# A scheduled one-core hybrid block: lag products with their sides exchanged, x's transposes issued ahead, powers on POOL

## The chip, the cores and the metric

The kernel runs on one core of a Trainium2 chip. The metric is the device time of one execution in microseconds. The engines are called as in the profile: PE (TensorE products), PEld (its weight loads), DVE (VectorE), ACT (ScalarE), POOL (GpSimd), SP (SyncE, which here only issues DMAs).

## The reference

One layer over 2048 tokens of 1024 channels, f32:

```python
hn = rmsnorm(h, mix_norm_g)
u, g_ssm, q, k, v, g_attn = split(hn @ w_in)          # 512 columns each
y_ssm = s5_branch(u, ...) * silu(g_ssm)               # 32 groups of 16 channels, 64 complex states
y_att = stick_breaking(q, k, v) * silu(g_attn)        # 8 heads of 64, strictly causal
h = h + concat(y_ssm, y_att) @ w_out
h = h + sigmoid(rmsnorm(h) @ w_ple_gate) * (p @ w_ple_proj)
```

`s5_branch` turns the complex poles `exp(a dt)`, the input matrix B and the output matrix C into a linear recurrence over time, then applies GELU and a gated linear unit. The change lies in u, in the gate product of `g_ssm` and in the preparation of the recurrence.

## The kernel before

**Products.** Large products are done in three f32r products of high and low halves (`split`, `mm3`): an operand's high part is written by ACT, the low part by DVE.

**u stage (`phase_u`).** T = 0 to 7 are blocks of 256 tokens. For T of 1 and more `load_x` fetches two halves of x, squares them on ACT (`jk`, sum into `ss`), makes the row factor `rs_x` (DVE L73, then a power on POOL, L501), scales x on ACT (L604), turns it by 64-row transposes on PE (`ps_x`, L520), splits the result into `xt` (ACT L507, DVE L66) and writes `xt` to memory as `hn`. T = 0 comes turned from the host. For T = 0 and 1 (`RAW = 2`) x is not scaled; `norms` computes the row factors (`ps_row`, `e.row`) and u is multiplied by them afterwards (L641, on POOL). The u product (`ps_u`) of a T has 96 PE products in four banks, which ACT copies to `uq` (L639).

**Preparation (`ssm_chain`, `ssm_pack`).** `ssm_chain` makes, on tiles with 32 columns, `dt`, `mag`, sine and cosine (`small_exp`, `small_sincos`), the powers of the pole (`pr`, `pi`, by `cmul` in doubling steps of 1, 2, 4, 8 times 32 columns), the scaled input matrices `bb` and `bbs` and the tables `tabs`. The tables' products run on POOL (`cmul` with `aside=True`), the rest on DVE. A pack (eight, four groups each) forms `bn` from the powers on DVE (128 x 1024), turns it on PE into `mb` (`stB`), and multiplies `bn` with C into `lags`, which goes to memory (`lag`) and comes back as a Toeplitz operand.

**Gate and state-space stage.** Packs, `ssm_batch` and `gate_unit` (product `ps_sg`, banks o and z0, evicted by ACT and DVE) run interleaved; the first attention projections run there too. Attention, gated linear unit and output follow.

**Order.** A planner in the file sets the order of every engine's instructions: `plan` collects operations and dependences, `duration` gives each a cost, `list_schedule` takes on each engine the ready operation of lowest rank, `best_order` repeats that with ranks from a backward pass and keeps the plan with the earliest end, `arrange` fixes it. Hints change it: `e.first` puts operations before all others, `e.later(T)` holds DMAs until the operation marked by `e.mark(T)` has begun, `e.abreast` keeps a group together. Engines run their queues strictly in that order on the chip, whatever is ready.

Of the kernel before, what the change touches and what calls it, by code (L numbers as in the profile page):

```python
# [8 lines left out]
F32 = mybir.dt.float32  # L9
# [4 lines left out]
ALU = mybir.AluOpType  # L14
# [4 lines left out]
P = 128  # L19
# [30 lines left out]
HOLD = 2  # L50
ACT0 = True
RAW = 2
MARK0, MARK1 = 7, 6
MATB = 1
GSB = 2
# [9 lines left out]
def vt(nc, out, a, b, op):  # L65
    nc.vector.tensor_tensor(out, a, b, op=op)  # L66
# [109 lines left out]
def ssm_chain(e, keep, sm):  # L176
# [35 lines left out]
    pr = R.pr = kt("pwr", [L + 1, G])  # L212
    pi = R.pi = kt("pwi", [L + 1, G])
# [4 lines left out]
    n = 1  # L218
    while n < L:
        bc = [a[:, n].unsqueeze(1).to_broadcast([P, n, G]) for a in (pr, pi)]  # L220
        cmul(e, sm, pr[:, n + 1:2 * n + 1], pi[:, n + 1:2 * n + 1], pr[:, 1:n + 1], pi[:, 1:n + 1], *bc, [n, G])
        n *= 2
    R.pis = kt("pwis", [L + 1, G])
    vs(nc, R.pis, pi, nsgn, ALU.mult)
# [79 lines left out]
def ssm_pack(e, sm, R, b):  # L304

    nc = e.nc
    gs = slice(b * GB, (b + 1) * GB)
    sh = [P, GB, L, GH]
    bn = sm.tile(sh, F32, tag="bn", name="bn")
    tm = sm.tile(sh, F32, tag="tm", name="tm")  # L310

    def pw(a, lo, rev):
        v = a[:, lo:lo + L, gs].rearrange("p t g -> p g t")
        if rev:
            v = v[:, :, ::-1]
# [12 lines left out]
    gp = nc.gpsimd.tensor_tensor  # L328
    gp(cview, pw(R.pr, 1, False), st(R.cts), op=ALU.mult)
    gp(tm2, pw(R.pi, 1, False), st(R.ct2), op=ALU.mult)  # L330
    gp(cview, cview, tm2, op=ALU.subtract)
    bnf = bn.rearrange("p g (s i) h -> p (g s) (i h)", s=HS)
    mbf = mb.rearrange("p g s m -> p (g s) m")
    for q in range(GB * HS // 4):
        ps = e.bank("ps_pack", "w0", "w1")
        for k in range(4):
            nc.tensor.transpose(ps[:, k * P:(k + 1) * P], bnf[:, 4 * q + k], e.ident)
        nc.scalar.activation(mbf[:, 4 * q:4 * q + 4].rearrange("p g m -> p (g m)"), ps, AF.Copy)
    ps = e.bank("ps_pack", "w0", "w1")
    for s in range(HS):  # L340
        for k in range(GB):
            o = (s * GB + k) * GH
            nc.tensor.matmul(ps[:, o:o + GH], bnf[:, HS * k + s], R.cts[:, b * GB + k, :], start=True, stop=True)
    lags = sm.tile([P, HS + 1, GB, GH], F32, tag="lags", name="lags", bufs=2)
    nc.vector.memset(lags[:, HS], 0.0)
    nc.scalar.activation(lags[:, :HS], ps[:, :HS * GB * GH].rearrange("p (s g h) -> p s g h", s=HS, h=GH), AF.Copy)
# [193 lines left out]
def phase_u(e, pool, xp, chain):  # L540
# [50 lines left out]
    def load_x(T):  # L591
        xt = xp.tile([P, 2, 2, NC8, P], F32R, tag="xg", name="xt", bufs=2)
        for hf in range(2):
            t0 = (2 * T + hf) * P
            x = pool.tile([P, DM], F32, tag="x", name="x", bufs=XB)
            nc.sync.dma_start(x, e.x[0, t0:t0 + P, :])
            jk = e.spare.tile([P, DM], BF16, tag="part", name="jk", bufs=1)
            ss = pool.tile([P, 1], F32, tag="ss", name="ss", bufs=2)
            nc.scalar.activation(jk, x, AF.Square, accum_out=ss)
            if T < RAW:  # L600
                sums.append(ss)
            else:
                rs = rms_rstd(e, pool, ss, 1, DM, "x")
                nc.scalar.activation(x, x, AF.Copy, scale=rs)  # L604
            for h, ps in enumerate(turned(e, "ps_x", ("tr", "ssm") if hf else ("z0", "z1"), [x[:, c * P:(c + 1) * P] for c in range(NC8)])):
                d = slice(64 * h, 64 * h + 64)
                split(e, xt[:, hf, 0, :, d], xt[:, hf, 1, :, d], ps)
            nc.sync.dma_start(e.hn_d[2 * T + hf], xt[:, hf].rearrange("p s c t -> p (s c t)").bitcast(F32))
        return xt

    xts = {}
    with e.first():
        xts[0], w = load_plain(0)
        with e.later(0):
            xts[1] = load_x(1)
        norms()
    prep = chain()
    for T in range(NT // 2):
        if 2 <= T + 1 < NT // 2:
            xts[T + 1] = load_x(T + 1)  # L620
        xt = xts.pop(T - 2, None)
        xt = xts[T]
        if T % 4 == 0:
            uq = [pool.tile([P, L, NCH // 2], F32, tag="uq", name="uq", bufs=5) for ct in range(4)]
        ps = [e.bank("ps_u", "w0", "w1", "o", "acc")[:, :256] for _ in range(4)]
        if T == 2:
            e.mark(T)
        if T == 1:
            e.mark(3)
        for ct, c in [(ct, c) for c in range(NC8) for ct in range(4)] if T == 0 else [(ct, c) for ct in range(4) for c in range(NC8)]:  # L630
            if T == 0 and ct == 0 and c == MARK1:
                e.mark(1)
            cs = slice(ct * P, (ct + 1) * P)
            mm3(e, ps[ct], (w[c][:, 0, cs], w[c][:, 1, cs]), (xt[:, :, 0, c], xt[:, :, 1, c]), c == 0, c == NC8 - 1)
        n = NCH // 8
        for ct in range(4):
            k0 = (T % 4) * n
            o, out = ps[ct].rearrange("p (c j) -> p j c", j=L), uq[ct][:, :, k0:k0 + n]
            nc.scalar.activation(out, o, AF.Copy)  # L639
            if T < RAW:  # L640
                nc.gpsimd.tensor_tensor(out, out, e.row[T].rearrange("p (c j) -> p j c", j=L), op=ALU.mult)  # L641
            if T % 4 == 3:
                c0 = (T // 4) * (NCH // 2)
                nc.gpsimd.dma_start(e.u_d[ct][:, :, c0:c0 + NCH // 2].rearrange("j p c -> p j c"), uq[ct])
# [3 lines left out]
def gate_unit(e, pool, w, T, xt):  # L648
# [390 lines left out]
def hybrid_block_kernel(ctx: ExitStack, tc: tile.TileContext, x, xt, small, p, w_in, ssm_w_glu, w_out, w_ple_gate,  # L1039
# [94 lines left out]
    def hint(kind):  # L1134
# [2 lines left out]
        yield  # L1137
        rows.append((n, len(nc.cur_bb.bb.instructions), kind))

    e.first, e.later, e.mark = (lambda: hint("first")), (lambda T=2: hint(T)), (lambda T: rows.append((len(nc.cur_bb.bb.instructions), T, "mark")))  # L1140
    e.rows, e.abreast = rows, abreast
    e.wpool = pool(ctx, "w", 16)
# [128 lines left out]
def duration(i, name, outs, ins, psum):  # L1271
# [232 lines left out]

def best_order(ops, pre, soft, length, mode, rows, turns=6):

    first, last, inner, soon = set(), set(), set(), set()
    hints = [r for r in rows if len(r) == 3]
    mark = {T: a for a, T, kind in hints if kind == "mark"}
    for a, b, kind in hints:  # L1510
        for k in range(a, b):
            if kind == "first":
                soon.add(k)
            elif kind in mark and type(ops[k]).__name__ == "InstDMACopy":
                soft[k].add(mark[kind])
    for a, b in [r for r in rows if len(r) == 2] + [(k, k + 2) for k, i in enumerate(ops) if type(i).__name__ == "InstRegisterMove"]:
# [10 lines left out]
        return [r - 1e6 if k in inner and k not in heads else r for k, r in enumerate(rank)]  # L1527

    for _ in range(turns):
        order, start, done = list_schedule(ops, pre, soft, length, mode, lead([k - 1e5 if k in soon else r for k, r in enumerate(rank)], first))  # L1530
# [67 lines left out]
```

## Time and profile before

| | |
|---|---|
| median of 3 runs | 1563.97 us (1562.64 to 1567.96) |
| profiled execution | 1565.11 us, span 1563.4 us |
| granted TensorE clock, mean | 0.984 |
| POOL, DVE, ACT busy | 844.9, 1057.6, 931.2 us |

A group row gives: line, engine, operation, output and inputs, shapes, count | busy us, mean ns of one | idle time of the engine before them and what ended it. A wait row gives: who waited for whom, us in total, times, longest. A timeline row gives: start, duration, engine, line, operation, count, and the idle time before it.

### The profile page before, as it was taken

To read this page: it belongs to the slowest core of one execution; us is meant where nothing else is said; L and a number is where in the kernel's file an instruction comes from. 1 tells how busy PE (TensorE), PEld (TensorE's weight loads), DVE (VectorE), ACT (ScalarE), POOL (GpSimd) and SP (SyncE) were. 2 spreads that over 40 slices of the span, in tenths; PEclk is the share of its full clock that TensorE was granted. 3 is DMA by queue.
4 is the path that set the end of the run, shared out by engine and by line. 5 is a ranking of instruction groups with operands and counts; after the bars stand their busy time and mean duration, and the time that the engine had idled before them with its cause. 6 is when DMAs were issued, how large, how long until landed. Compare 5 with 4: busy or idle time off the path is not lost.

```text
span 1563.4 us, 34915 instructions
## 1 busy us (share of the span) xinstructions
PE 1484.2 (95%) x13120; PEld 1261.9 (81%) x13120; DVE 1057.6 (68%) x1953; ACT 931.2 (60%) x2069; POOL 844.9 (54%) x1131
## 2 busy tenths in 40 slices
PE   8899999889999999998999988999999999999998
PEld 7899989878888888887888876777776888777776
DVE  7845868657677877678768785666869556754544
ACT  6553545456677877677867777666765435633432
POOL 3843433435556666565666598774565654433433
PEclk9999999999999999999999998999999999999999
DMA  8767636454332422334223365763347645622211
GB/s 334 273 248 216 205 109 208 147 182 157 139 110 95 134 94 95 108 116 136 91 89 116 127 222 167 234 181 95 104 147 252 200 162 182 196 68 93 89 61 61
DMA packets 168377, 236.22 MB, mean 151 GB/s; under 512 B 63504, under 2 KB 109712, under 8 KB 156816
## 3 DMA queue, kind: packets, MB, share of 16 engines
q1 hardware_dynamic: 166272, 226.50, 44.4%
q0 software_dynamic: 1936, 7.49, 1.7%
q8 instruction: 104, 1.70, 0.5%
q14 instruction: 65, 0.53, 0.1%
HBM read 169.05 MB, written 64.90 MB: 150 GB/s over the span
## 4 chain that ended last, share of the span: by engine, by line
PE 77%; DVE 8%; ACT 5%; issue 4%; POOL 3%; DMA 2%; POOLq 0%; SPq 0%; ACTq 0%; DVEq 0%
PE ps_q L744 20%; PE ps_o L848 6%; PE ps_z L809 6%; PE ps_wt L520 4%; PE ps_g L713 3%; PE ps_g L715 3%; PE ps_h L713 3%; PE ps_h L714 3%; PE ps_g L714 3%; PE ps_h L715 3%; DVE px L825 2%; DMA wst<-in_ssm_w_glu_dram 1%; PE ps_sg L535 1%; PE ps_u L535 1%; PE ps_u L536 1%
## 5 line engine op out<-in xcount | busy, mean ns | idle before, releaser
L827 POOL TENSOR_TENSOR be<-be,px 128x512 f32<-128x512 f32 (+3 forms) x320 | 317.3, 996 | 205.8 <-DVE px L825 157.2
L744 PE MATMUL ps_q<-w_w,xt 64*128 64x512 f32 x2880 | 406.1, 404 | 11.4 <-DVE v L66 9.7
L825 DVE TENSOR_TENSOR_SCAN px<-px,ps_z 128x512 f32<-128x512 f32 (+3 forms) x320 | 339.8, 1086 | 103.5 <-ACT be L819 73.8
L744 PEld LDWEIGHTS ps_q<-w_w,xt 64*128 64x128 f32 x2880 | 297.5, 187 | 52.8 <-issue 9.5
L814 ACT ACTIVATE px<-ps_z 128x512 f32<-128x512 f32 (+3 forms) x320 | 162.8, 540 | 76.9 <-PE ps_z L809 58.8
L840 ACT ACTIVATE ws<-ps_wt 128x512 f32<-128x512 f32 (+3 forms) x320 | 164.9, 550 | 62.7 <-PE ps_wt L520 62.4
L819 ACT ACTIVATE be<-ps_z 128x512 f32<-128x512 f32 (+3 forms) x320 | 167.8, 555 | 0.5 <-PE ps_wt L520 0.5
L809 PE MATMUL ps_z<-k,q 64*128 64x512 f32 (+3 forms) x960 | 148.9, 384 | 14.0 <-DVE px L825 11.1
L848 PE MATMUL ps_o<-ws,v 128*64 128x128 f32 x2176 | 140.1, 281 | 1.0 <-ACT ws L840 1.0
L848 PEld LDWEIGHTS ps_o<-ws,v 128*64 128x64 f32 x2176 | 120.3, 139 | 19.6 <-issue 15.6
L520 PEld LDWEIGHTS ps_wt<-ident,be 64*128 64x128 f32 x2176 | 104.5, 142 | 28.8 <-POOL be L827 8.9
L809 PEld LDWEIGHTS ps_z<-k,q 64*128 64x128 f32 x960 | 97.1, 189 | 33.3 <-DVE px L825 17.3
L520 PE MATMUL ps_wt<-ident,be 64*128 64x64 f32 x2176 | 111.5, 229 | 8.0 <-ACT ws L840 3.2
L1020 POOL TENSOR_TENSOR sg<-sg,h 128x512 f32<-128x512 f32 x32 | 44.8, 1411 | 114.3 <-DVE sg L66 114.3
L501 POOL TENSOR_TENSOR rs_qk<-rs_qk,mhalf 128x4 f32<-128x4 f32 x64 | 65.7, 1027 | 42.4 <-DVE rs_qk L73 41.6
L535 PE MATMUL ps_u<-xt,w_w 128*128 128x256 f32 x256 | 75.9, 297 | 6.6 <-ACT w_w L485 6.1
L536 PE MATMUL ps_u<-xt,w_w 128*128 128x256 f32 x256 | 75.4, 295 | 2.1 <-DVE xt L66 2.1
L66 DVE TENSOR_TENSOR yr<-sx,yr 128x512 fp32r<-128x512 f32 x64 | 53.4, 854 | 34.9 <-ACT yr L507 34.1
L823 POOL TENSOR_SCALAR_AFFINE_SELECT px<-px 128x128 f32<-128x128 f32 x128 | 39.4, 318 | 69.1 <-ACT px L814 67.5
L537 PE MATMUL ps_u<-xt,w_w 128*128 128x256 f32 x256 | 74.6, 294 | 0.0
L507 ACT ACTIVATE yr<-sx 128x512 fp32r<-128x512 f32 x64 | 39.3, 628 | 52.1 <-POOL sx L906 20.5
L1014 ACT ACTIVATE sg<-sg,rs 128x512 f32<-128x512 f32 x24 | 17.4, 725 | 74.0 <-DVE sg L66 74.0
(421 smaller groups left out, 3694.9 us busy)
## 6 DMA issues: line engine op xcount, KB each, us to landing
xt<-hn SPq DMA_DIRECT2D x60, 1024.0 KB, 4.9
hn<-xt SPq DMA_DIRECT2D x16, 1024.0 KB, 8.5
h<-h SPq DMA_DIRECT2D x64, 256.0 KB, 3.5
wst<-in_w_in_dram SPq DMA_DIRECT2D x48, 256.0 KB, 5.5
xg<-hn SPq DMA_DIRECT2D x12, 1024.0 KB, 7.0
out_dram<-sg SPq DMA_DIRECT2D x32, 256.0 KB, 2.5
x<-in_x_dram SPq DMA_DIRECT2D x14, 512.0 KB, 6.5
h<-in_x_dram SPq DMA_DIRECT2D x28, 256.0 KB, 4.4
```

Of the source, the lines that this page charges most:

```text
L520: e.nc.tensor.transpose(ps[h][:, 64 * k:64 * k + 64], v[r], e.ident[r, r])
L535: mm(out, wh, xh, start=first, stop=False)
L713: mm(out, xh, wh, start=first, stop=False, skip_group_check=more)
L714: mm(out, xh, wl, start=False, stop=False, skip_group_check=more)
L744: nc.tensor.matmul(o, xt[r, a, c], A.w[c][r, b], start=c + s == 0, stop=c == NC8 - 1 and s == 2)
L809: nc.tensor.matmul(z[:, :n], q[half[h], a], A.k[ch][half[h], b, :n], start=s == 0, stop=s == 2)
L814: nc.scalar.activation(px[:, :n], z[:, :n], AF.Sigmoid, scale=-(HD ** -0.5))
L819: nc.scalar.activation(be[:, :n], z[:, :n], AF.Sigmoid, scale=HD ** -0.5)
L825: nc.vector.tensor_tensor_scan(rv, rv, z[:, :n][:, ::-1], initial=1.0 if carry[h] is None else carry[h], op0=ALU.mult, op1=ALU.bypass)
L827: nc.gpsimd.tensor_tensor(be[:, :n], be[:, :n], px[:, 1:n + 1], op=ALU.mult)
L840: nc.scalar.activation(dst, ps, AF.Copy)
L848: nc.tensor.matmul(po[half[h], :P], A.v[sb][:, h], w[:, h, b], start=sb == i, stop=sb == 0)
```

## The change

- **Lag products** (`ssm_pack`): instead of eight products with `bn` stationary (128 x 128) and 16 columns of C moving, four with 32 columns of C stationary (a group and its neighbour; the neighbour's half is not used) and 256 columns of `bn` moving, each into 32 rows of the bank, kept together by `abreast`; ACT copies the result to `lt`, two transposes turn it, ACT copies every other 16 columns to `lags`. The pack's banks are w0 alone.
- **x's transposes and splits** (`load_x`) get a hint `ahead`: their rank is lowered by `LEAD = 12` us in the planner.
- **`norms`** is no longer in the group that `first` puts before all others.
- **Powers**: within `ssm_chain`, all products and sums of two tensors behind sine and cosine go to POOL.
- **Row factors**: DVE multiplies by them; for T = 1 straight from the bank, without ACT's copy.
- **Later loads**: DMAs under `later()` wait for T = 4 instead of T = 2 (gate weights, small constants, first attention weights).
- **Gate**: banks o, z0 and w1.
- **Planner's cost** of a product with 32 or fewer output rows is halved.

```diff
+LEAD = 12
+LATER = 4
@@ ssm_chain
+    R.ct = ct
     dt, x1, mag, th, sn, cs = (t(s) for s in ("dt", "x1", "mag", "th", "sn", "cs"))
-    vt(nc, x1, lr, dt, ALU.mult)
+    nc.vector.tensor_tensor(x1, lr, dt, op=ALU.mult)
-    vt(nc, th, li, dt, ALU.mult)
+    nc.vector.tensor_tensor(th, li, dt, op=ALU.mult)
     small_sincos(e, sm, sn, cs, th, G)
+
+    def vt(nc, out, a, b, op):
+        nc.gpsimd.tensor_tensor(out, a, b, op=op)
...
-        cmul(e, sm, ..., [n, G])
+        cmul(e, sm, ..., [n, G], True)
@@ ssm_pack
-        ps = e.bank("ps_pack", "w0", "w1")
+        ps = e.bank("ps_pack", "w0")
...
-    ps = e.bank("ps_pack", "w0", "w1")
+    ps = e.bank("ps_pack", "w0")
+    flat = R.ct.rearrange("p k g h -> p (k g h)")
+    with e.abreast():
+        for k in range(GB):
+            o = (b * GB + k) * GH
+            nc.tensor.matmul(ps[2 * GH * k:2 * GH * (k + 1), :HS * P], flat[:, o:o + 2 * GH], bnf[:, HS * k:HS * (k + 1)].rearrange("p s m -> p (s m)"), start=True, stop=True)
+    lt = sm.tile([P, HS * P], F32, tag="lt", name="lt")
+    nc.scalar.activation(lt, ps[:, :HS * P], AF.Copy)
+    ps = e.bank("ps_pack", "w0")
     for s in range(HS):
-        for k in range(GB):
-            o = (s * GB + k) * GH
-            nc.tensor.matmul(ps[:, o:o + GH], bnf[:, HS * k + s], R.cts[:, b * GB + k, :], start=True, stop=True)
+        nc.tensor.transpose(ps[:, s * P:(s + 1) * P], lt[:, s * P:(s + 1) * P], e.ident)
...
-    nc.scalar.activation(lags[:, :HS], ps[:, :HS * GB * GH]..., AF.Copy)
+    nc.scalar.activation(lags[:, :HS], ps[:, :HS * P].rearrange("p (s g v h) -> p s g v h", s=HS, v=2, h=GH)[:, :, :, 0], AF.Copy)
@@ phase_u
+            with e.ahead():
+                (transposes and splits of load_x)
-        norms()            # inside e.first()
+    norms()                # behind it
-        if T == 2:
-            e.mark(T)
+        if T == LATER:
+            e.mark(2)
-            nc.scalar.activation(out, o, AF.Copy)
+            if T != 1:
+                nc.scalar.activation(out, o, AF.Copy)
             if T < RAW:
-                nc.gpsimd.tensor_tensor(out, out, e.row[T]..., op=ALU.mult)
+                vt(nc, out, o if T else out, e.row[T]..., ALU.mult)
@@ gate_unit
-        o = e.bank("ps_sg", "o", "z0")[:, :256]
+        o = e.bank("ps_sg", "o", "z0", "w1")[:, :256]
@@ duration
-        return (1 if half else 2) * max(cols / 1160.0, 0.056), 0.12
+        return (0.5 if outs[0][0] <= 32 else 1 if half else 2) * max(cols / 1160.0, 0.056), 0.12
@@ best_order
+            elif kind == "ahead":
+                ahead.add(k)
-        ... lead([k - 1e5 if k in soon else r for k, r in enumerate(rank)], first))
+        ... lead([k - 1e5 if k in soon else r - LEAD if k in ahead else r for k, r in enumerate(rank)], first))
```

More of the change, by code (lines that the diff above doesn't have):

```diff
@@ L220, in ssm_chain @@
         bc = [a[:, n].unsqueeze(1).to_broadcast([P, n, G]) for a in (pr, pi)]
-        cmul(e, sm, pr[:, n + 1:2 * n + 1], pi[:, n + 1:2 * n + 1], pr[:, 1:n + 1], pi[:, 1:n + 1], *bc, [n, G])
+        cmul(e, sm, pr[:, n + 1:2 * n + 1], pi[:, n + 1:2 * n + 1], pr[:, 1:n + 1], pi[:, 1:n + 1], *bc, [n, G], True)
         n *= 2
@@ L604, in load_x @@
                 nc.scalar.activation(x, x, AF.Copy, scale=rs)
-            for h, ps in enumerate(turned(e, "ps_x", ("tr", "ssm") if hf else ("z0", "z1"), [x[:, c * P:(c + 1) * P] for c in range(NC8)])):
-                d = slice(64 * h, 64 * h + 64)
-                split(e, xt[:, hf, 0, :, d], xt[:, hf, 1, :, d], ps)
+            with e.ahead():
+                for h, ps in enumerate(turned(e, "ps_x", ("tr", "ssm") if hf else ("z0", "z1"), [x[:, c * P:(c + 1) * P] for c in range(NC8)])):
+                    d = slice(64 * h, 64 * h + 64)
+                    split(e, xt[:, hf, 0, :, d], xt[:, hf, 1, :, d], ps)
             nc.sync.dma_start(e.hn_d[2 * T + hf], xt[:, hf].rearrange("p s c t -> p (s c t)").bitcast(F32))
@@ L638, in phase_u @@
             o, out = ps[ct].rearrange("p (c j) -> p j c", j=L), uq[ct][:, :, k0:k0 + n]
-            nc.scalar.activation(out, o, AF.Copy)
+            if T != 1:
+                nc.scalar.activation(out, o, AF.Copy)
             if T < RAW:
-                nc.gpsimd.tensor_tensor(out, out, e.row[T].rearrange("p (c j) -> p j c", j=L), op=ALU.mult)
+                vt(nc, out, o if T else out, e.row[T].rearrange("p (c j) -> p j c", j=L), ALU.mult)
             if T % 4 == 3:
@@ L1138, in hint @@
         rows.append((n, len(nc.cur_bb.bb.instructions), kind))
+    e.ahead = lambda: hint("ahead")
     e.first, e.later, e.mark = (lambda: hint("first")), (lambda T=2: hint(T)), (lambda T: rows.append((len(nc.cur_bb.bb.instructions), T, "mark")))
@@ L1505, in best_order @@
 def best_order(ops, pre, soft, length, mode, rows, turns=6):
-    first, last, inner, soon = set(), set(), set(), set()
+    first, last, inner, soon, ahead = set(), set(), set(), set(), set()
     hints = [r for r in rows if len(r) == 3]
@@ L1529, in best_order @@
     for _ in range(turns):
-        order, start, done = list_schedule(ops, pre, soft, length, mode, lead([k - 1e5 if k in soon else r for k, r in enumerate(rank)], first))
+        order, start, done = list_schedule(ops, pre, soft, length, mode, lead([k - 1e5 if k in soon else r - LEAD if k in ahead else r for k, r in enumerate(rank)], first))
         if best is None or max(done) < best[0]:
```

1 line of the change is left out of this document (removed).

## The prediction

> **What bounds the kernel now.** I read the page first, then the stretches that the diff touches as windows, then what TensorE (PE) waits for in each of them.
>
> ```profile
> span 1563.4 us, 34915 instructions
> ...
> PE 1484.2 (95%) x13120; PEld 1261.9 (81%) x13120; DVE 1057.6 (68%) x1953; ACT 931.2 (60%) x2069; POOL 844.9 (54%) x1131
> ```
>
> PE is busy for 95% of the span. Time comes out of this kernel in two ways only: less work on PE, or fewer gaps on it. The windows (columns: stretch, its length, busy time of PE, PEld, DVE, ACT, POOL with counts, granted clock, DMA share, GB/s) divide the part that the diff touches into the u stage (0 to 131 us) and the gate and state-space stage (131 to 330 us):
>
> ```profile
> 0.00:131.00 131.00, 116.59 (x1044) 113.42 (x1044) 83.58 (x246) 69.36 (x127) 79.33 (x145) 0.96 0.75 270
> 131.00:330.00 199.00, 188.29 (x1478) 181.27 (x1476) 142.97 (x273) 96.82 (x220) 65.30 (x41) 0.98 0.56 174
> ```
>
> PE idles 14.4 us in the first and 10.7 us in the second. These are the waits behind it, first stage and second stage:
>
> ```profile
> PE ps_u L535 <- ACT w_w L485: 6.1, 1, 6.1
> PE ps_x L520 <- ACT x L604: 4.4, 2, 4.2
> PE ps_u L536 <- DVE xt L66: 2.1, 1, 2.1
> PE ps_row L586 <- DVE xt L66: 1.1, 1, 1.1
> PE ps_u L535 <- ACT xt L507: 0.5, 1, 0.5
> ```
>
> ```profile
> PE ps_sg L535 <- DVE sg L66: 2.7, 3, 1.5
> PE ps_pack L337 <- DVE bn L66: 2.5, 2, 1.8
> PE ps_pack L343 <- ACT stB L338: 1.5, 2, 1.3
> ```
>
> The 6.1 us are the first load, which nothing here touches. The others are what can be won, and a gap can cost more than itself, as the granted clock shows just behind them:
>
> ```profile
> 20.00:30.00 10.00, 8.70 (x75) 8.16 (x75) 8.01 (x37) 8.32 (x19) 4.79 (x8) 0.83 1.01 417
> 40.00:50.00 10.00, 7.38 (x47) 7.18 (x48) 8.90 (x50) 3.99 (x7) 8.85 (x33) 0.83 0.93 307
> 70.00:80.00 10.00, 5.82 (x65) 5.43 (x64) 8.48 (x17) 4.37 (x9) 9.72 (x22) 0.93 1.02 348
> 80.00:90.00 10.00, 10.00 (x91) 9.67 (x91) 5.13 (x11) 5.55 (x10) 7.49 (x17) 0.90 0.87 314
> ```
>
> 0.83 over 10 us is 1.7 us of clock lost; 0.93 and 0.90 together are again 1.7 us. So each of the three stalls of the u stage (ps_row, then xt, then x) drags 1.7 us behind it.
>
> **The lag products.** A pack multiplies eight times with the 128-wide bn stationary and 16 columns of cts moving; each product is two instructions. The change makes four products with 32 columns of ct stationary and 256 columns of bn moving, put side by side into the four 32-column strips, then one more eviction and two whole transposes.
>
> ```profile
> L391 PE MATMUL ps_b<-us,stB 128*128 128x128 f32 x128 | 16.4, 278 | 0.0
> L343 PE MATMUL ps_pack<-cts,bn 128*128 128x16 f32 x128 | 15.6, 259 | 1.5 <-ACT stB L338 1.5
> L639 ACT ACTIVATE uq<-ps_u 128x256 f32<-128x256 f32 x32 | 11.8, 384 | 33.7 <-PE ps_u L537 33.6
> L337 PE MATMUL ps_pack<-ident,bn 128*128 128x128 f32 x64 | 10.2, 292 | 2.5 <-DVE bn L66 2.5
> L848 PE MATMUL ps_o<-ws,v 128*64 128x128 f32 x2176 | 140.1, 281 | 1.0 <-ACT ws L840 1.0
> ```
>
> The 16-column product pays as much as a 128-column one: 15.6/128 = 0.122 us an instruction against 16.4/128 = 0.128 (L391). Before: 16 x 0.122 = 1.95 us a pack, 15.6 in eight packs. L848 shows two 64-wide strips abreast: 140.1/2176 = 0.064 us, half. No row has four strips of 32. The new eight instructions move 256 columns, so 0.256 us each one after another (2.05 a pack), 1.02 two abreast, 0.51 four abreast. The two transposes cost 2 x 10.2/64 = 0.32. Then the array changes its form twice a pack; the u stage shows that price:
>
> ```profile
> 17.85 0.28 PE L536 MATMUL ps_u<-xt,w_w 128*128 128x256 f32 x1
> 17.97 0.28 PE L537 MATMUL ps_u<-xt,w_w 128*128 128x256 f32 x1
> 18.18 0.71 PE L520 MATMUL ps_x<-ident,x 64*128 64x64 f32 x16
> 18.83 0.39 PE L535 MATMUL ps_u<-xt,w_w 128*128 128x256 f32 x1
> 19.05 0.28 PE L536 MATMUL ps_u<-xt,w_w 128*128 128x256 f32 x1
> ```
>
> Products of one form start 0.12 us apart (17.85, 17.97); over the borders it is 0.21 (into the half-height transposes) and 0.22 (19.05 behind 18.83). So 0.1 us a border, 0.2 a pack. The Trainium skill, "TensorEngine Tiling (Array Packing)", Key Properties, holds that changing the tiling mode drains the array, which speaks against this edit; the trace agrees and makes it small. A pack then costs 0.51 + 0.32 + 0.2 = 1.03, gain 0.92, **-7.4 us** in eight. Ends: two abreast 1.54 a pack, -3.3; no overlap 2.57, +5.0. I take four abreast, since the nearest row (L848) shows strips running fully beside each other. The Trainium skill, "TensorE: Matmul & The Clock Gate", Measured speedup vs the span model, reports 2.38x for three 32-column strips; with that factor the products would take about 0.86 and the gain be an estimated 4.6 instead of 7.4; no run here shows it. The extra eviction is 0.38 us of ACT (L639), 3 us in eight packs beside ACT's 97 busy of 199; on PE it hides under gate products. All four fills of a pack now share one bank, w0, so each waits for the eviction before it. By the rows above two evictions of 512 columns (about 0.8 each), two of 256 (0.38) and the fills make an estimated 4 us a pack, 32 of 199: hidden under gate products, and at most that much where PE has none.
>
> **The gate's third bank.** ps_sg waited 2.7 us in three places for DVE to empty a bank. A third bank lets the next product start: **-2 us** (ends -2.7 and 0).
>
> **The u stage.** (a) The norms leave the "first" group. PE then no longer waits at ps_row (1.1) and keeps its clock (1.7): **-2.8**. What is late next:
>
> ```profile
> L641 POOL TENSOR_TENSOR uq<-uq,row x8: 850/868/897, 27.4 to 40.5; 128x256 f32<-128x256 f32 x8
> ...
> L575 ACT ACTIVATE row<-ps_row x4: 264/278/279, 25.1 to 30.1; 128x128 f32<-128x128 f32 x4
> ```
>
> T = 1's banks are now emptied by DVE times the row factor, so a late factor holds banks that T = 2 wants. The last factor came at 30.1 and the last row product at 40.5: 10 us of cover. (b) ps_u waited 0.5 + 2.1 for the split of T = 2's x on DVE. "Ahead" lifts transposes and both split instructions by 12 us in rank, and DVE loses work. I take half the idle time and the clock, 1.3 + 1.7: **-3.0** (0 to -4.3). (c) The longest stall:
>
> ```profile
> 74.34 0.81 POOL L172 TENSOR_TENSOR cp<-tabs 128x32 f32<-128x32 f32 x1
> ...
> 75.11 1.19 POOL L644 DMA_DIRECT2D u<-uq  x1
> ...
> 76.32 0.81 POOL L501 TENSOR_TENSOR rs_x<-rs_x,mhalf 128x1 f32<-128x1 f32 x1
> ...
> 77.17 1.15 ACT L604 ACTIVATE x<-x,rs_x 128x1024 f32<-128x1024 f32 x1 [4.04 <-POOL rs_x L501]
> ...
> 78.37 1.02 PE L520 MATMUL ps_x<-ident,x 64*128 64x64 f32 x16 [4.18 <-ACT x L604]
> ```
>
> The transposes sat in PE's queue 4.2 us before x was scaled, because its factor waited on POOL behind table products and a DMA issue. "Ahead" covers transposes and splits, not that factor. It goes only if the new order puts POOL's work elsewhere. Stall and clock are 5.9; I take half, **-3.0** (0 to -5.9).
>
> **Powers to POOL, row factors to DVE.**
>
> ```profile
> L173 POOL TENSOR_TENSOR tabs<-tabs,cp 128x256 f32<-128x256 f32 x2 | 1.8, 904 | 0.0
> ...
> L173 POOL TENSOR_TENSOR tabs<-tabs,cp 128x32 f32<-128x32 f32 x4 | 1.2, 300 | 0.2
> ```
>
> ```profile
> L437 POOL TENSOR_TENSOR swp<-swp,tabs 128x512 f32<-128x512 f32 x8 | 10.6, 1322 | 35.1 <-ACT swp L413 30.5 <-DVE gsq L77 4.5
> ```
>
> POOL takes 33 products of 32 or 64 columns at about 0.3, 12 of 128 or 256 at 0.3 to 0.9 (say 0.7), 6 of 512 at 1.3: 10 + 8 + 8 = 26 us; it gives up eight row products of 0.87 (L641), 7 us. Net +19 on an engine that is 97% busy from 70 to 80 us. The powers are first used for bn, which PE takes up much later:
>
> ```profile
> L337 PE MATMUL ps_pack<-ident,bn x64: 270/273/448, 129.7 to 298.6; 128*128 128x128 f32 x64
> L66 DVE TENSOR_TENSOR bn<-pwr,bb x8: 1206/1224/2244, 89.3 to 283.6; 128x1024 f32<-128x1024 f32 x8
> ```
>
> From 89.3, where the first bn began, to 129.7 are 40 us, which cover 19 more: 0 on the path by this use. If that cover is gone, each us late is a us of PE. DVE gives up 51 products for eight: 0.
>
> **Later loads.** Gate weights and small constants are held until T = 4 instead of T = 2. Eight T share the 125 us behind the first load, so T = 4 begins near 68 us:
>
> ```profile
> L480 SPq DMA_DIRECT2D wst<-in_w_in_dram x10: 333/570/1147, 43.4 to 138.8; - x10
> L485 ACT ACTIVATE w_w<-wst,gmix x8: 712/718/755, 66.6 to 134.6; 128x512 fp32r<-128x512 f32 x8
> ```
>
> They were fetched in pairs from 43.4 us; two staging buffers make each pair wait for the split of the one before. In SP's queue x's loads then stand in front of them. From 68 us four pairs must be split before the gate near 120, 13 us each; I take 0, and the first pairs no longer share the DMA engines (0.93 busy from 40 to 50) with x.
>
> **Sum.** -7.4 - 2 - 2.8 - 3 - 3 = -18.2. With less PE work the stage from 131 to 330 leans on DVE's chain (143 busy of 199; waits on bn 2.5 above), so I give back a third of that stage's 9.4: +3. Net -15.2. Behind 330 us the order is worked out anew by the same planner without a change of work: 0, give or take 5. The profiled execution took 1565.1 us (span 1563.4), 1.1 over the median of the runs: 1565.1 - 15.2 - 1.1 = 1549.
>
> **Rivals.**
> 1. All stalls named above go: -2.8 - 4.3 - 5.9 - 7.4 - 2.7 = -23.1, 1541. For it: all have one cause, order. Against: (c)'s factor is not moved ahead. Chance 0.15.
> 2. Slower: POOL's queue delays x's factor (rs_x). Transposes moved ahead sit in PE's queue in front of products that could run, as in (c), and POOL now has 19 us more to do. It decides once the factor lags over 1 us behind its place in the plan, since PE then stands and its clock falls. If (c) stays, (b) is not won and three more such stalls of 5.9 come: -2.8 + 17.7 - 7.4 - 2 + 3 = +8.5, 1572. For it: 9.72 of 10 busy. Against: in the kernel before, with much the same queue, PE's ps_x waited for x twice only, 4.4 us in all. Chance 0.13. The Trainium skill, "GPSIMD Engine Reference", Engine selection, sends two-input elementwise work to VectorE and calls GpSimd about twice as slow, which is the rule behind this rival; no run shown so far has the powers on POOL.
> 3. Gate weights late: pairs keep their pace of (134.6 - 66.6)/3 = 23 us, the last split comes 25 us later (68 for 43), and PE lacks, as an estimate, half of that as other work, 12, with 1.7 of clock: -15.2 + 13.7, 1562. Chance 0.10.
> 4. The strips do not run abreast: +5.0 for -7.4, 1561. Chance 0.10.
>
> **How the numbers follow.** Forecast 0.50, rivals 0.15, 0.13, 0.10, 0.10, other 0.02. About 0.3% (4.7 us) is what a measurement of this kernel can tell. Forecast and rival 1 are below 1559.3, and a part of 3 and 4: faster 0.70. The rest of 3 and 4 and the forecast's upper edge: same 0.15. Rival 2 and spill: slower 0.15. The range runs from just under rival 1 to above 3 and 4: 1536 to 1568; rival 2 is left out.
>
> **What would show it.** Right: no gap over 1 us on PE from 20 to 110 us, granted clock 1.00 there; a pack's lag products under 1.1 us with transposes; waits of ps_sg on DVE sg near 0; the gate's last split before 120. Wrong: PE's ps_x waiting for ACT x behind POOL rs_x more than once (rival 2), ps_sg waiting for ACT w_w by many us (3), new products starting 0.2 us apart (4), or the gap total of 131 to 330 growing by what the packs save.

## The result: no measurable change

The changed kernel took 1563.58 us (median of 12 runs, 1561.42 to 1566.96), the kernel before 1564.68 (12 runs beside them): ratio 0.9992, 95% interval 0.9977 to 1.0007. The forecast was 1549. In the changed kernel helper lines are shifted by 2 (L66 is L68, L77 is L79), the others by up to 14: scaling of x is L616, its transposes L532, its factor L513, the u product L547 to L549, lag products L350 and L355 (ACT's copy between them L352).

The profiled execution took 1561.99 us. Its page, and the two stretches as windows (columns as before):

```profile
span 1560.3 us, 34808 instructions
...
PE 1478.4 (95%) x13072; PEld 1248.0 (80%) x13072; DVE 1048.7 (67%) x1910; ACT 932.2 (60%) x2073; POOL 856.5 (55%) x1174
```

```profile
0.00:131.00 131.00, 113.86 (x1015) 109.58 (x1016) 59.52 (x201) 65.39 (x120) 80.73 (x183) 0.97 0.73 263
131.00:330.00 199.00, 185.78 (x1467) 172.65 (x1465) 157.41 (x277) 102.69 (x235) 79.87 (x50) 0.99 0.59 184
```

PE has less work, yet its last gate product starts only 1.8 us earlier (327.1 for 328.9): its idle time grew from 14.4 to 17.1 us in the u stage and from 10.7 to 13.2 in the gate stage. What it waited for, first in the u stage, then in the gate stage:

```profile
PE ps_x L532 <- ACT x L616: 9.2, 7, 3.4
PE ps_u L547 <- ACT w_w L497: 6.1, 1, 6.1
PE ps_row L598 <- DVE xt L68: 1.0, 1, 1.0
```

```profile
PE ps_sg L549 <- DVE w_w L79: 4.0, 2, 3.3
PE ps_qk L727 <- DVE gsq L68: 1.9, 2, 1.3
PE ps_pack L343 <- ACT stB L344: 1.5, 2, 1.0
PE ps_sg L547 <- DVE sg L68: 1.4, 1, 1.4
```

The split of x (2.1 and 0.5 before) no longer holds PE up, but the waits for x itself went from 4.4 us in two places to 9.2 in seven, and the gate now waits 4.0 us for DVE's part of its weights, for which it did not wait before. Of the three losses of granted clock in the u stage one is gone, and two came back later:

```profile
20.00:30.00 10.00, 8.58 (x85) 7.47 (x83) 8.49 (x50) 8.86 (x19) 3.71 (x9) 1.00 1.00 395
40.00:50.00 10.00, 8.69 (x84) 8.42 (x83) 7.58 (x22) 4.76 (x9) 8.98 (x27) 1.00 0.51 184
70.00:80.00 10.00, 10.00 (x83) 9.66 (x83) 2.64 (x5) 5.89 (x12) 9.98 (x21) 0.83 0.99 305
100.00:110.00 10.00, 9.96 (x83) 9.66 (x80) 6.65 (x10) 4.03 (x9) 5.61 (x11) 0.83 0.47 173
```

**The lag products did nearly what was forecast.** Gate stage, the kernel before and then the changed one; both timelines of PE:

```profile
298.95 1.87 PE L343 MATMUL ps_pack<-cts,bn 128*128 128x16 f32 x16
300.67 0.36 PE L535 MATMUL ps_sg<-xg,w_w 128*128 128x256 f32 x1
300.87 0.28 PE L536 MATMUL ps_sg<-xg,w_w 128*128 128x256 f32 x1
```

```profile
178.51 0.28 PE L547 MATMUL ps_sg<-xg,w_w 128*128 128x256 f32 x1
178.72 0.64 PE L350 MATMUL ps_pack<-bn,cts 128*32 128x256 f32 x8
179.29 0.39 PE L548 MATMUL ps_sg<-xg,w_w 128*128 128x256 f32 x1
179.51 0.39 PE L467 MATMUL ps_y<-rot,stC 128*128 128x127 f32 x2
...
307.07 0.38 PE L355 MATMUL ps_pack<-ident,lt 128*128 128x128 f32 x2
307.20 0.36 PE L548 MATMUL ps_sg<-xg,w_w 128*128 128x256 f32 x1
307.41 0.28 PE L549 MATMUL ps_sg<-xg,w_w 128*128 128x256 f32 x1
```

The gate product behind such a group is itself followed late (300.67 to 300.87, 179.29 to 179.51, 307.20 to 307.41, for 0.12 us elsewhere), so I count up to the second start behind the group and take off 0.12 for each gate product in between. Before, a pack's products took 300.87 - 298.95 - 0.12 = 1.80 us of PE. Now 178.51 to 179.51 is 1.00, less 0.24 for two gate products: 0.76 with both borders; the transposes 307.41 - 307.07 - 0.12 = 0.22. Together 0.98, a gain of 0.82 a pack and 6.6 in eight; the forecast's term was 7.4. In the trace's records four products on four strips start 6 to 7 ns apart, and the second four 0.24 us behind the first.

**x's factor did not.** One of the ten places, timeline of the changed kernel (PE's u products and all weight loads left out):

```profile
95.98 0.75 DVE L73 TENSOR_SCALAR tabs<-tabs,pr_sgn 128x512 f32<-128x512 f32 x1 [4.19 <-POOL cp L174]
96.20 0.64 POOL L175 TENSOR_TENSOR pr_t22i<-pr_t22i,cp 128x32 f32<-128x32 f32 x1
96.65 0.13 DVE L75 TENSOR_SCALAR rs_x<-ss 128x1 f32<-128x1 f32 x1
96.81 0.23 POOL L173 TENSOR_TENSOR pr_t24r<-pr_t22r 128x32 f32<-128x32 f32 x1
97.00 0.34 POOL L174 TENSOR_TENSOR cp<-tabs,pr_t22i 128x64 f32<-128x64 f32 x1
97.31 0.34 POOL L173 TENSOR_TENSOR tabs<-tabs,pr_t22i 128x64 f32<-128x64 f32 x1
97.61 0.55 POOL L513 TENSOR_TENSOR rs_x<-rs_x,mhalf 128x1 f32<-128x1 f32 x1
...
98.19 1.15 ACT L616 ACTIVATE x<-x,rs_x 128x1024 f32<-128x1024 f32 x1 [4.94 <-POOL rs_x L513]
...
99.39 0.40 PE L532 MATMUL ps_x<-ident,x 64*128 64x64 f32 x6 [3.44 <-ACT x L616]
```

ACT stands 4.94 us before scaling x, and the transposes stand at the head of PE's queue for 3.44. The factor is late in two queues. Its first step, on DVE (L75), starts at 96.65, behind a sign product of the tables that itself had stood 4.19 us for a table product of POOL. Its second step, on POOL (L513), then stands 0.83 us behind short table products. Taken from the timelines for all twelve factors, the time from the end of x's squares to the DVE step, and from that step to POOL's, adds up to 14.1 and 7.7 us in the kernel before and to 21.8 and 14.4 in the changed one. How much of the first is POOL's doing, as it is in the place shown, is not separated. Over the stage, ACT's waits for this factor, which the view puts down to the last step alone, the kernel before and then the changed one:

```profile
ACT x L604 <- POOL rs_x L501: 11.2, 5, 4.0
```

```profile
ACT x L616 <- POOL rs_x L513: 25.0, 10, 5.1
```

**A balance up to the gate's end.** I counted PE's instructions up to the start of the last gate product and gave each the steady spacing of its form (0.12 us for 256 columns, 0.11 for 128); what remains of the time is "excess": the first load, waits, borders and clock. Work: 288.8 us before, 280.0 after (-8.8; borders count as excess). Gate's end: 328.9 before, 327.1 after. Excess: 40.1 before, 47.1 after. So 7 of the 8.8 us were lost again, 3.6 in the u stage and 3.3 in the gate stage. Of the 3.3, some 2.2 are the new products' own borders (8.8 without them, 6.6 with them by the timelines above), so that about 1 is left there for waits and clock. Up to the gate's end all orders have the same work but for the lag products; ahead of u's end they have different numbers of gate products (36 before, 24 after), so u's end alone compares two orders roughly. The last three columns of this table come from the profiled executions, all counted in the same way:

| kernel | median us | ratio (95%) | u's end | gate's end | excess to there |
|---|---|---|---|---|---|
| before | 1564.7 | 1 | 130.9 | 328.9 | 40.1 |
| after | 1563.6 | 0.9992 (0.9977 to 1.0007) | 133.0 | 327.1 | 47.1 |
| lag products alone | 1564.8 | 0.9997 (0.9987 to 1.0006) | 129.8 | 330.1 | 50.1 |
| + third gate bank | 1558.3 | 0.9960 (0.9945 to 0.9974) | 132.3 | 324.9 | 44.9 |
| + POOL's prices | 1550.4 | 0.9898 (0.9878 to 0.9918) | 119.9 | 311.9 | 31.9 |
| before, POOL's prices | 1562.8 | 0.9980 (0.9968 to 0.9991) | 120.3 | 322.7 | 33.9 |
| after, POOL's prices | 1560.6 | 0.9976 (0.9966 to 0.9986) | 123.4 | 321.8 | 41.8 |

### The profile page after: what moved, and what is told of

Same layout as the page of the kernel before. It is cut to its first block, busy times and chain, and to the rows that moved or that the text cites. A ratio compares the mean times of both kernels' runs of the same rounds, so it can differ in the third digit from the quotient of the medians.

```text
span 1560.3 us, 34808 instructions
## 1 busy us (share of the span) xinstructions
PE 1478.4 (95%) x13072; PEld 1248.0 (80%) x13072; DVE 1048.7 (67%) x1910; ACT 932.2 (60%) x2073; POOL 856.5 (55%) x1174
## 5 line engine op out<-in xcount | busy, mean ns | idle before, releaser
L532 PEld LDWEIGHTS ps_wt<-ident,be 64*128 64x128 f32 x2176 | 103.7, 141 | 30.9 <-POOL be L841 10.2
L532 PE MATMUL ps_wt<-ident,be 64*128 64x64 f32 x2176 | 110.0, 227 | 9.5 <-ACT ws L854 5.0
L513 POOL TENSOR_TENSOR rs_qk<-rs_qk,mhalf 128x4 f32<-128x4 f32 x64 | 64.9, 1014 | 44.2 <-DVE rs_qk L75 36.4
L547 PE MATMUL ps_u<-xt,w_w 128*128 128x256 f32 x256 | 76.1, 298 | 6.1 <-ACT w_w L497 6.1
L68 DVE TENSOR_TENSOR yr<-sx,yr 128x512 fp32r<-128x512 f32 x64 | 53.6, 859 | 34.4 <-ACT yr L519 33.7
L549 PE MATMUL ps_u<-xt,w_w 128*128 128x256 f32 x256 | 74.4, 293 | 0.0
L79 DVE SCALAR_TENSOR_TENSOR w_w<-wst,gmix,w_w 128x512 fp32r<-128x512 f32 x48 | 47.4, 999 | 25.6 <-ACT w_w L497 25.2
```

The source lines that it names most:

```text
L532: e.nc.tensor.transpose(ps[h][:, 64 * k:64 * k + 64], v[r], e.ident[r, r])
L547: mm(out, wh, xh, start=first, stop=False)
```

## The experiments

Each ran 4 to 12 times beside the kernel before. That kernel's median lay between 1564.7 and 1565.8 us from one session to the next, so ratios compare two experiments better than medians do.

**The change undone in parts.** First the powers back on DVE, then the hint without its 12 us, then the loads held until T = 2 as before.

```diff
-        nc.gpsimd.tensor_tensor(out, a, b, op=op)          # ssm_chain, vt
+        nc.vector.tensor_tensor(out, a, b, op=op)
-        cmul(..., [n, G], True)
+        cmul(..., [n, G])
```

> The changed kernel with the powers, the input matrices' products and the decay products back on DVE; all else as changed. Theory A (x's factor waits on POOL behind the powers moved there): ACT's waits for rs_x on POOL fall from 25.0 us towards the 11.2 of before, PE's waits of ps_x for x fall from 9.2 to about 4, the last u product starts near 128 instead of 132.9, and the time is about 5 us under the changed kernel's 1563.6 (1558). Theory B (the hint ahead alone is at fault, it puts the transposes in front of ready products): ps_x still waits about 9 us and the time stays within 2 us of 1563.6.

1561.53, 0.9973 (0.9961 to 0.9986): 2 us under the changed kernel by medians, 3 by ratios, but the intervals overlap. PE's waits for x fell from 9.2 to 6.8 us, ACT's for the factor from 25.0 to 19.8: the powers are a part of the delay, not the whole.

```diff
-LEAD = 12
+LEAD = 0
```

> The changed kernel with a lead of 0 for x's transposes and splits. Theory B: PE's waits of ps_x for x fall from 9.2 us to 4 or less, the u stage ends 5 us sooner, time near 1558. Theory A: the factor is as late as before on POOL (ACT waits for rs_x near 25 us); PE runs u products meanwhile but then lacks xt, so its idle time in the first 131 us stays near 17 us and the time within 2 us of 1563.6.

1569.61, 1.0021 (1.0008 to 1.0033), u's end at 141.4. So the hint is no harm in this order: without it the kernel is slower, by 6 us in medians and 4.5 in ratios, which neither theory expected.

```diff
-LATER = 4
+LATER = 2
```

> The changed kernel with the later loads held until T = 2 as before, all else as changed. If the later loads cost what the u stage or the early gate loses (PE waits 4.9 us for the gate's weights behind 131 us in the changed kernel): those waits fall to 1.5 or less and the time is 3 to 5 us under 1563.6. If holding them back is what keeps DMA and ACT free for x: PE's waits in the u stage grow by 3 or more and the time is 3 to 6 us over. If neither: within 2 us.

1563.63, 0.9992 (0.9983 to 1.0000): no difference. PE's waits for x were 11.2 us in seven places: early loads do not bring them about, late ones do not cure them.

**Parts put on the kernel before.** The lag products alone (the lines of `ssm_pack` and `duration` in the change), then also the third bank.

> The kernel before with the lag products alone exchanged (one bank for the pack and the planner's cost of narrow products included). If the pack's 7.5 us of PE work, as its trace now shows, come through by themselves: near 1557.5 against 1564.7 of before, and the gate's last product starts 7 us sooner than 328.9. If the gate and state-space stage gives them back (theory D: its chain on DVE and ACT is as long as PE's work): 1562 or more, with PE's idle time from 131 to 330 us up by 5 or so from 10.7.

1564.83, 0.9997: 8.8 us of PE's work (6.6 with the borders) are gone and nothing is won. Its waits in the gate stage:

```profile
PE ps_pack L350 <- ACT lt L347: 5.9, 5, 2.0
PE ps_sg L542 <- DVE sg L66: 4.9, 3, 2.4
```

```diff
-        o = e.bank("ps_sg", "o", "z0")[:, :256]
+        o = e.bank("ps_sg", "o", "z0", "w1")[:, :256]
```

> The kernel before with the lag products exchanged and the gate on three banks, nothing else. With the lag products alone PE waited 5.9 us for the new eviction lt and 4.9 us for the gate's banks, and the time was that of before. If the missing third bank is why the pack's 7.5 us did not come through: both waits fall to 3 us together, the gate's last product starts near 323 and the time is about 6 us under before (1559). If the stage's own chain takes them back whatever the banks: waits move elsewhere, last product at 328 or later, time within 2 us of before.

1558.34, 0.9960 (0.9945 to 0.9974): about 6 us less by one bank (6.5 by medians, 0.37% by ratios). The wait for `lt`, 5.9 above, is 1.0 here, that for `sg` is 2.1. As I read it, the pack's chain through one bank needs other products to cover it, and PE has them only when the gate is free to go on.

**x's factor.** First without it: x of T = 2 to 7 is scaled by a constant, so the row normalization of these blocks is left out.

```diff
-                nc.scalar.activation(x, x, AF.Copy, scale=rs)
+                nc.scalar.activation(x, x, AF.Copy, scale=0.9)
```

> The changed kernel with x scaled on ACT by a constant instead of its row factor for T = 2 to 7 (the row normalization of those tokens is left out); the factor is still computed but nobody waits for it. Theory A: PE's waits of ps_x for x go (under 2 us), the last u product starts 8 to 10 us sooner than 132.9, and the time falls by 6 to 10 us to 1554 to 1558. If what is won in the u stage is given back at its end by the gate's weights or by the state-space chain (theory C): the u stage ends sooner, but the gate's last product is within 3 us of 327, and the time within 3 us of 1563.6.

1558.50, 0.9959 (0.9944 to 0.9973): PE's waits for ACT's x are gone and 5 us with them. u's end came at 127.6 for 133.0, but the 24 gate products that lay before it now lie behind it; counted as in the table, the excess up to u's end fell by 2.9 us. 6.4 us of waits for the split of x (4.0 and 2.4) came in place of the 9.2, and the waits for DVE's part of the gate's weights grew from 4.0 to 5.8.

Then the hint extended to squares, factor and scaling of x:

```diff
+            with e.ahead():
                 nc.scalar.activation(jk, x, AF.Square, accum_out=ss)
...
                     rs = rms_rstd(e, pool, ss, 1, DM, "x")
                     nc.scalar.activation(x, x, AF.Copy, scale=rs)
```

> The changed kernel with the hint ahead over the whole path of x's row factor too (squares, the DVE step, POOL's power, ACT's scaling), not over transposes and splits alone. If the failing point is that the factor was not moved ahead with the transposes (theory A, by priority): PE's waits of ps_x for x fall from 9.2 to under 3 us, the u stage ends 4 to 6 us sooner than 132.9, time near 1558. If POOL's load, not its order, makes the factor late: waits above 7 us, time within 2 us of 1563.6.

1562.88, 0.9984 (0.9974 to 0.9994); ACT's waits for the factor stayed at 25.8 us in ten places, and PE's for x grew to 10.7 in nine. The planner does not see the delay, so a higher rank changes little. It gives a two-tensor product on POOL 0.12 us + 1.86 ns a column, so 0.18 for 32 columns, and a DMA issue 0.6; the rows above show 0.23 to 0.34 for short products with 0.64 now and then, and the prediction's row L644 shows 1.19. Over dozens of such steps POOL runs microseconds behind its plan. So the prices were set to what the traces show:

```diff
-        return (0.6 if eng == "Pool" else 0.45), 0.0
+        return (1.2 if eng == "Pool" else 0.45), 0.0
-            return 0.35 + 0.15 * n, 0.08
+            return 0.45 + 0.15 * n, 0.08
+        if name == "InstTensorTensor" and n <= 256:
+            base, slope = 0.18, 0.0028
```

> The changed kernel with the planner's costs on POOL set to what the traces show (a two-tensor product of 32 columns 0.27 us, 256 columns 0.90 us, a DMA issue 1.2 us, the factor's power 0.6 us); no work is moved by hand. Theory A in its sharper form (the factor is late because POOL runs behind the plan, 30 to 45% longer than the plan thinks on small products): the plan now fits, ACT's waits for rs_x fall from 25.0 to under 12 us, PE's waits of ps_x from 9.2 to under 4, time 3 to 6 us under 1563.6. If POOL is simply overloaded there, whatever the plan: waits stay above 8 us and the time within 2 us.

u's end moved from 133.0 to 123.4, PE's waits for x from 9.2 us to 0.3, with no change of work. POOL's queue, which had held the twelve factors for 14.4 us, holds them for 1.9, and the time ahead of their DVE step is 12.8 for 21.8: most of the delay comes from the planner's wrong prices for POOL, though ACT still waits 9.4 us for the factor. Which of the three prices does it was not tried, and they mend more than this one wait, for the excess up to u's end fell by 11.8 us where leaving the factor out had taken off 2.9. The whole kernel won only 3 us, 1560.58, 0.9976 (0.9966 to 0.9986), for the gate then stood 11.2 us in one place. From the timeline there POOL, DVE and PE's waiting product:

```profile
125.73 2.04 POOL L335 TENSOR_TENSOR stC<-pwr,cts 128x1024 f32<-128x1024 f32 x1
126.32 7.78 DVE L68 TENSOR_TENSOR lags<-lags,dg 32x64 f32<-32x64 f32 x1 [1.15 <-ACT lags L358]
127.73 2.01 POOL L336 TENSOR_TENSOR tm<-pwi,cts 128x1024 f32<-128x1024 f32 x1
129.71 2.01 POOL L335 TENSOR_TENSOR stC<-pwr,cts 128x1024 f32<-128x1024 f32 x1
131.68 2.33 POOL L337 TENSOR_TENSOR stC<-stC,tm 128x1024 f32<-128x1024 f32 x1
134.09 2.02 POOL L336 TENSOR_TENSOR tm<-pwi,cts 128x1024 f32<-128x1024 f32 x1
134.14 2.05 DVE L68 TENSOR_TENSOR dg<-ident,abd 32x64 f32<-32x64 f32 x1
...
136.22 3.51 DVE L79 SCALAR_TENSOR_TENSOR w_w<-wst,gmix,w_w 128x512 fp32r<-128x512 f32 x2
...
139.13 0.58 PE L549 MATMUL ps_sg<-xt,w_w 128*128 128x256 f32 x1 [11.20 <-DVE w_w L79]
```

A DVE product of 64 columns lasts 7.78 us, ending 0.1 us behind the fourth POOL product in a row; the same step takes 0.22 elsewhere. Behind it stand the splits of the gate's weights. The page "SBUF — State Buffer" of the Trainium skill, section "SBUF: two separate sides", says that a DVE operation with two SBUF inputs and a GpSimd operation that reads SBUF contend for one pair of ports: whichever starts first has it for its whole instruction, and the other blocks fully. The trace agrees: POOL's product began at 125.73, DVE's at 126.32, and here DVE stood through four instructions in a row. The changed kernel itself has the same, beside POOL's products at 133.61 and 135.61 (2.05 and 2.02 us): DVE's splits between 130 and 145 us, and PE's wait for the first of them:

```profile
L79 DVE SCALAR_TENSOR_TENSOR w_w<-wst,gmix,w_w x3: 752/3617/4544, 133.6 to 145.0; 128x512 fp32r<-128x512 f32 x3
```

```profile
138.24 0.52 PE L549 MATMUL ps_sg<-xt,w_w 128*128 128x256 f32 x2 [3.34 <-DVE w_w L79]
```

**What holds the gate once x is on time.** Two theories on e6's 11.2 us: POOL's products block DVE (P), or the loads held until T = 4 come too late (C). Three edits on the kernel with POOL's prices: powers on DVE (as above), the pack's three products on POOL replaced by one ACT copy (which leaves the output matrix out of `stC`), and `LATER = 2`. The second of them:

```diff
-    gp(cview, pw(R.pr, 1, False), st(R.cts), op=ALU.mult)
-    gp(tm2, pw(R.pi, 1, False), st(R.ct2), op=ALU.mult)
-    gp(cview, cview, tm2, op=ALU.subtract)
+    nc.scalar.activation(cview, pw(R.pr, 1, False), AF.Copy)
```

The results in the order of the edits:

> The changed kernel with the planner's POOL costs as the traces show and the powers back on DVE. With these costs alone the u stage ended at 123.4, but PE then waited 11.2 us for the gate's weights, whose DVE step stood behind DVE instructions of 32 x 64 elements that took 7.8 and 2.1 us while POOL ran pack products of 128 x 1024 without a break. Theory P (powers on POOL push POOL's pack products into the time in which DVE must make the gate's weights, and DVE instructions with two SBUF inputs stand still meanwhile): the wait for the weights falls under 3 us, time 1553 to 1556. If the weights are late from their later loads (theory C): they still cost 8 us or more and the time stays near 1560.

1555.70, 0.9940 (0.9927 to 0.9954).

> The changed kernel with the measured POOL costs, powers still on POOL, but each pack's three products of 128 x 1024 on POOL left out and replaced by one ACT copy of the first factor (the state's output matrix is wrong). Theory P: with them gone no DVE instruction of 32 x 64 takes over 1 us from 110 to 160 us, the wait for the gate's weights falls from 11.2 us to under 3, time 1550 to 1554. Theory C: the weights are waited for by 8 us or more all the same, time near 1560.

1550.27, 0.9907 (0.9892 to 0.9921). Splits of the gate's weights on DVE between 100 and 200 us, the kernel with POOL's prices and then this one (minimum, median, maximum in ns):

```profile
L79 DVE SCALAR_TENSOR_TENSOR w_w<-wst,gmix,w_w x14: 740/1020/2850, 104.3 to 188.7; 128x512 fp32r<-128x512 f32 x14
```

```profile
L79 DVE SCALAR_TENSOR_TENSOR w_w<-wst,gmix,w_w x14: 742/750/941, 105.6 to 178.8; 128x512 fp32r<-128x512 f32 x14
```

> The changed kernel with the measured POOL costs and the later loads at T = 2 again. Theory C (the later loads make the gate's weights late): the wait of 11.2 us for them falls under 3 us, the u stage still ends near 123 to 126, time 1552 to 1556. Theory P: waits of 6 us or more remain (DVE stands behind POOL's pack products whenever the loads land), time 1558 to 1562.

1552.45, 0.9915 (0.9899 to 0.9931), no wait of the gate for weights left. Each theory missed once: P had 1558 to 1562 for the earlier loads, C 1560 without POOL's pack products. So both hold: the splits are hurt because they come late and because POOL runs then. Taking away either is worth 8 to 11 us, against 5 for the powers on DVE, with which POOL's pack products began at 111.0 instead of 125.7 us.

**The best version.** Lag products, third bank and POOL's prices on the kernel before, without the rest of the change:

> The kernel before with the lag products, the gate's third bank and the planner's POOL costs as the traces show them; powers and row factors stay where they were, no lead, later loads at T = 2. Theory A (plan too short on POOL makes x's factor late): the u stage's waits of ps_x for x (4.3 us with lag products and bank alone) fall under 1.5 and its end from 132.3 to 127 or less; with the gate stage unchanged 3 to 5 us under the 1558.3 of lag products and bank (1554). If the gate's weights take it back: within 2 us of 1558.

1550.42, 0.9898 (0.9878 to 0.9918). The longest waits of PE in its u stage beside the first load:

```profile
PE ps_sg L544 <- DVE w_w L77: 3.1, 2, 1.8
PE ps_row L593 <- DVE xt L66: 1.1, 1, 1.1
```

Three runs asked what in this belongs to the change. POOL's prices alone on the kernel before:

> The kernel before with the planner's POOL prices alone (short two-input products 0.18 us + 2.8 ns a column, power 0.45, DMA issue 1.2 us). Theory A, the fault was there before: x's factor waits on POOL there too (11.2 us of ACT behind it, a stall of 4.2 on PE), so the right prices take 4 to 8 us off: 1556 to 1560, and PE's waits for x go to near 0. Rival, the prices matter only where PE has less work to hide behind or POOL has the powers as well: 1562 to 1566, no change.

1562.79, 0.9980 (0.9968 to 0.9991). The fault was there before the change: waits for x are gone (ACT's for the factor 1.2 us), u's end moved from 130.9 to 120.3. But at the gate's end only 6.2 us of it were left, and 3 in the median. Behind the gate the profiled execution took 1240.6 us for 1234.5 before, with the same work. The two stretches as windows, before and then this kernel:

```profile
328.90:1563.40 1234.50, 1179.62 (x10603) 967.26 (x10601) 832.12 (x1437) 765.46 (x1724) 700.30 (x946) 0.99 0.42 135
322.70:1563.30 1240.60, 1187.24 (x10603) 970.61 (x10601) 834.84 (x1437) 766.82 (x1724) 700.23 (x946) 0.98 0.42 134
```

PE has the same products and idles no more (54.9 and 53.4 us), but is busy 7.6 us longer at a lower granted clock, 0.98 for 0.99 (in the records behind that column 23.5 us of clock are lost there, for 17.1): what was won at the gate's end went into the clock. Part of that may be chance, since this execution is 2.2 us above its kernel's median; the granted clock over all executions, 0.9795 in the median for 0.982 beside them, points the same way. Why less clock was granted stays open. Prices alone and lag products with bank alone win 0.2% and 0.4%; together 1.0%.

The best version with the hint on x's transposes:

> Lag products, third gate bank and POOL's prices, and with them the hint on x's transposes and splits (LEAD = 12). Theory A, nothing is left for the hint: PE has no wait for x without it, so 1550 +- 2. Rival, the hint also frees the split of x and starts products earlier: 1545 to 1547. Third possibility, the transposes stand in front of products that could run: 1553 or more and new waits for ACT x.

1554.85, 0.9929 (0.9912 to 0.9947), so rather slower. There is no wait for x that the hint could remove; u's end came earlier (117.5), but without 35 of the 36 gate products that lay before it, and then the next pack's `bn` met POOL's products:

```profile
122.66 5.66 DVE L67 TENSOR_TENSOR bn<-pwr,bb 128x1024 f32<-128x1024 f32 x1 [11.93 <-PE ps_pack L346]
```

That is 5.66 us for a step of 1.22, and PE waited 5.6 for it. And the whole change with the right prices, but powers on DVE and `LATER = 2`:

> The whole change with POOL's prices, but the powers on DVE and the loads held until T = 2. Theory A, powers on POOL and later loads are all that takes the gain back: 1548 to 1551, as lag products, third bank and prices alone. Rival, the rest of the change (row factors on DVE, norms later, the hint) costs something of itself: 1553 to 1556.

1553.89, 0.9918 (0.9901 to 0.9935). Against 1550.4 of the best version the intervals overlap: whether the rest of the change costs anything stays open. How far the time scatters between orders that differ in nothing of substance was not measured either, so steps of 2 or 3 us between two orders may be no more than that.

## Why the prediction was wrong

Up to the gate's end the forecast was -15.2 us; it came to -1.8. By its terms:

- **Lag products, -7.4: right in kind, a little too large.** 6.6 from the rows: strips fully abreast, 0.76 with both borders for the forecast 0.71, but the old products took 1.80 and not 1.95. Rival 4 is out. The 2.38x for three strips of the Trainium skill's "TensorE: Matmul & The Clock Gate", Measured speedup vs the span model, was no limit here for four: the estimated 2.05 by 0.76 is 2.7 with both borders in it. That the estimated 4 us a pack through bank w0 hide under gate products held only with the third bank: without it the whole gain was lost.
- **Third bank, -2: under-sized.** ps_sg's waits on `sg` fell from 2.7 to 1.4, but the bank's true worth is what it lets PE do in the packs' waits, about 6 us between the two experiments on the kernel before.
- **(a) -2.8 and (b) -3.0: half right.** Clock 1.00 at 20 to 30 and 40 to 50 us as forecast, split of x no wait any more; but the wait at ps_row stayed (1.0), this time with no loss of clock beside it, so a stall need not drag 1.7 us of clock behind it; and two of the three losses came back at 70 and 100 us behind waits for x.
- **(c) -3.0: the step that failed.** "It goes only if the new order puts POOL's work elsewhere": it did not, and the waits went from 4.4 to 9.2 us. The term also looked at POOL's queue alone: of the delay of the factor in the stall shown there 2.35 us lay ahead of its DVE step and 2.63 in POOL's queue, and over all twelve factors both grew with the change (14.1 to 21.8 and 7.7 to 14.4). With it all three u-stage terms fell: forecast -8.8, measured excess +3.6. Rival 2 (0.13) named the mechanism and its sign of failure (ps_x waiting for x more than once) but priced it as three stalls of 5.9; it came as seven waits, the longest 3.4.
- **Powers to POOL, 0: wrong.** The working asked when the powers are used (40 us of cover) and not what stands behind them in POOL's queue: x's factor, and the packs' POOL products, which stood at 126 to 144 us and there held DVE's splits. Powers on DVE were worth 2 to 3 us as the change stands, which is not clear of noise, and 5 with the right prices.
- **Later loads, 0: right as the change stands** (no difference with `LATER = 2`), presumably because x was late anyway; wrong by 8 us or more with the right prices. Rival 3's place was right (ps_sg waits for w_w 4.0, 11.2 with the prices); its cause was only half the loads.
- **Given back, +3: right by idle time** (10.7 to 13.2 us from 131 to 330), though through weights rather than through bn.
- **Behind 330 us, 0 give or take 5: right.** 1234.5 before, 1233.2 after.

The premise below (c) was the deeper fault: 9.72 of 10 us busy was read as a full engine, while the row showed short products at 0.3 to 0.8 us and an issue at 1.2. Compared with the planner's own 0.18 and 0.6 they say that POOL runs behind any plan. That comparison was to be had before the run.

## What to carry to other kernels

Where a planner fixes the order, compare its price of each short step with the trace before trusting any plan: an engine that is late by 0.1 us a step over fifty steps can hold every engine that waits for its one small result. A step moved to another engine is costed by what stands behind it there, not only by who uses it. Work taken off the critical engine pays only if that engine has something else ready in the gaps: here, on the kernel before, one more bank decided over all of it.

## What was not expected of the hardware

DVE products with two SBUF inputs do not share with POOL's 128 x 1024 products but stand until POOL pauses: 7.78 us for a step of 0.22, 5.66 for one of 1.22, 4.54 for a split of 0.75. Products with one input in a bank did not suffer: with POOL's prices `gsq<-gsq,ps_y` (L79, 128 x 512) took 670 to 675 ns four times, although POOL's products ran beside it. Four strips of 32 columns start 6 to 7 ns apart, so eight f32 products of 256 columns take 0.76 us with both changes of form. The forecast had strips abreast from two to four; it had nothing on DVE standing still.
